# Hybrid decoder layer on one core: q and k blocks split in one operation and placed by DMA, weight sums by accumulating loads, gate and branch products in another order, output projection by single token tiles

## Chip, cores and metric

One core of one Trainium2 chip runs the whole layer. The metric is the device time of one execution in microseconds (us). Engines are named as in the profile: PE (TensorE), ACT (ScalarE), DVE (VectorE), POOL (GpSimd), SP (SyncE, which issues DMA transfers only here).

## The reference

One layer, float32, 512 tokens of width 1024, 256 memory tokens.

```
h = rms_norm(x, g_mix);  proj = h @ w_in            # q,k,v of two mixers, forget logits, memory q, 3 gates
y_m = moba_attention(rope(norm(q_m)), rope(norm(k_m)), v_m)     # 8 heads of 64, blocks of 256
y_f = fox_attention(norm(q_f), norm(k_f), v_f, cumsum(log_f))   # 8 heads of 64
y_c = memory_attention(norm(q_c), norm(k of mem), v of mem)     # 4 heads of 128
merged = sigmoid(a_m)*(y_m @ w_br_moba) + sigmoid(a_f)*(y_f @ w_br_fox) + sigmoid(a_c)*(y_c @ w_br_mem)
x = x + merged @ w_out
h2 = rms_norm(x, g_ffn)
x = x + (silu(h2 @ w_gate) * (h2 @ w_up)) @ w_down
```

With 512 tokens MoBA has two blocks, so its top-3 choice takes every past block and the attention is plainly causal.

## The kernel before

**Number format.** Every factor of a product is split into a high part, rounded to a narrow format on ACT (`w_hi`, `qT` first half), and a low part, the rest, by a subtraction on DVE (`w_lo`). A product is three matmuls (`PASSES`: high by high, high by low, low by high). q, k and v of the heads of 64 use another layout: a `qT` or `kT` slot holds high and low parts on two sets of 64 partitions, so that a score needs two matmuls over 128 partitions.

**Weights.** `pieces` lists the weight pieces of 512 x 256 (512 KB) in order of use. `load_next` (L161) loads one into a `w_raw` slot by SP; a piece of kind "pair" is loaded by SP and a second source is added onto it by an accumulating DMA that POOL issues (L169). The order of the loads is by `due`, or three pieces ahead (`RAW_AHEAD`). `split_next` (L185) makes the parts: the first `HALVES` (8) pieces in two halves, each with its own ACT and DVE operation, the later ones whole. `take` (L234) hands the split pieces to a product.

**Units by seven products.** Three units of 512 columns (K and Q of four MoBA heads, V, K and Q of the other four; `plan_unit`, L100) are computed by `tok_unit` (L666) in seven half-size products M1, M2, M5, M6, M3, M7, M4, whose left factors are weight pieces or sums of them: S1 is a "pair"; S2 (S1 plus the first piece of the unit) and S4 (S2 plus the second) are of kind "sum", added by DVE (`w_sum`, L197).

**Order of the work.** The order is written out by hand for all engines. PE's stream of large products passes through `mm` (L272); each time about 1.3 us of columns have been issued, `tick` (L257) puts the next bit of everything else into the queues: one weight split, the callbacks whose count has run out (`later(n, fn)`: n ticks), and steps of a list `side` at a given rate per tick (`beside(steps, rate)`). A `tick` comes after 7 matmuls of 512 columns or 13 of 256. `flush_side` (L279) runs all steps that are left, with no product between them; `branch_part` calls it when an attention's output is still missing.

**Heads.** After its product a group of four heads is normalised and rotated on POOL (`head_rest`), then `turn_pair` (L528) transposes a block of two heads into PSUM by four PE transposes, and evacuates it: ACT writes the high part of each head (L543, 64 partitions), DVE the low part of each (L547, 64 partitions). For q the four quarters lie crosswise in one slot; for k each head has a slot of its own, of which POOL doubles 64 partitions onto the other 64 by DMA a tick later (L551, L552). `attention` (L850) then runs 16 groups per call in steps: scores (PE, L858), negated minimum and mask (DVE, L869), exponential (ACT, L887), scaling of `p_t` (POOL, L891), transposes (PE, L909), split of `pt` (ACT L298, DVE L301), values (PE, L920), y (ACT L927, DVE L928), and, after the last of a pair, the split of `yT`. The memory attention (L776) is built alike; its scaling is at L804, its transposes at L815.

**Gates and branches.** `gate_part` (L983) computes a chunk of 256 gate columns and its tanh on ACT (with a load of ACT's function table, `use_table`, L63, where the set changes); `branch_part` (L993) projects the attention's output and multiplies; branch 1 adds to `acc` on POOL (L1012). `gate_chunk` is one after the other. The starts of the four attentions are the calls `later(n, lambda: beside(attention(...), rate))` at L1031, L1039, L1112 and L1122.

**Output projection.** For column chunks 0 and 1, `out_pair` (L1215) runs two token tiles at once, the last of the eight contraction tiles at the end, into two of the three "m" banks of PSUM; chunks 2 and 3 go by `out_group`. `out_sum` (L1205) adds x on DVE (L1208) and squares on ACT (L1210). The switch of the function table for the second norm stands ahead of it all (L1197). The feed-forward part behind it (L1153 to L1473) isn't touched.

Of the kernel before, what the change touches and what calls it, by code (L numbers as in the profile page):

```python
# [12 lines left out]
F32R = mybir.dt.float32r  # L13
# [6 lines left out]
NT = S // P  # L20
# [17 lines left out]
def f32(ap):  # L38
    return ap.bitcast(F32)
# [3 lines left out]
def hybrid_layer(ctx, tc, rope, x, mem, g_mix, w_in, b_forget, g_q_moba, g_k_moba, g_q_fox,  # L43
# [12 lines left out]
    def slot(name, dt=F32):  # L56
        return U.tile([P, SLOT], dt, name=name, tag="u", bufs=NSLOT)
# [42 lines left out]
    def plan_unit(col1, col2):  # L100

        i = len(pieces)
        a = {(c, kh): cols(w_in, kh, DIN, (col1, col2)[c], 256) for c in range(2) for kh in range(2)}
        pieces.extend([("load", a[0, 0], 4, 256), ("load", a[0, 1], 4, 256),
                       ("pair", (a[1, 0], a[1, 1]), 4, 256), ("sum", (i + 2, i), 4, 256),
                       ("sum", (i + 3, i + 1), 4, 256),
                       ("pair", (a[1, 0], a[0, 0]), 4, 256), ("load", a[1, 1], 4, 256)])
        due.update({i + 2: i - 5, i: i - 4, i + 1: i - 3, i + 5: i - 2, i + 6: i + 3})

    DIN = w_in.shape[2]  # L110
    for c in (0, 256):
# [12 lines left out]
    def plan_gates(a, wb, chunks):  # L124
        for c in chunks:
            plan_gate(a, c)
            plan_branch(wb, c)
# [10 lines left out]
    plan_cols(w_in, D, DIN, V_F + 256, 264)  # L138
    plan_cols(w_in, D, DIN, K_F + 256, 256)
    plan_cols(w_in, D, DIN, Q_F + 256, 256)  # L140
    plan_gates(A_M, w_br_moba, (0, 1))
    for b in (K_F, Q_F, V_F):
        plan_cols(w_in, D, DIN, b, 256)
    plan_gates(A_M, w_br_moba, (2, 3))
# [3 lines left out]

    raws, split, used = {}, {}, {}
    st = {"load": 0, "split": 0, "take": 0, "stage": 0}  # L150
    HALVES = 8
    RAW_AHEAD = 3
    loads = sorted((i for i, piece in enumerate(pieces) if piece[0] != "sum"),
                   key=lambda i: due.get(i, i - RAW_AHEAD))
# [6 lines left out]
    def load_next():  # L161
        i = loads[st["load"]]
        st["load"] += 1
        kind, src, nk, w = pieces[i]
        r = raws[i] = slot("w_raw")
        dst = r[:, :nk * w].rearrange("p (k c) -> p k c", k=nk)
        if kind == "pair":
            nc.sync.dma_start(dst, src[0])
            nc.gpsimd.dma_start(dst, src[1], accum_op=OP.add)  # L169
        else:  # L170
            nc.sync.dma_start(dst, src)

# [322 lines left out]
    def head_rest(raw, ss, ntok, d, kind, gc, dst, blk0, lag, rows=None, e=2, gains=None):  # L495
# [32 lines left out]
        def turn_pair(blk):  # L528
            tb = bank("a")
            for tt in range(ntok):  # L530
                pe.transpose(tb[:, tt * P:(tt + 1) * P],
                             raw[:, tt * 256 + blk * P:tt * 256 + (blk + 1) * P], ident)
            if gc in (GQM, GQF):
                o = slot("qT", F32R)
                dst[blk0 + blk] = o
                o2 = [(o[:, 0:512], o[:, 0:512]), (o[:, 512:1024], o[:, 512:1024])]
            else:
                ks = [slot("kT", F32R), slot("kT", F32R)]
                dst[blk0 + blk] = ks
                o2 = [(k[:, 0:512], k[:, 512:1024]) for k in ks]  # L540
            for h, (hi, lo) in enumerate(o2):
                r = slice(64 * h, 64 * h + 64)
                act.activation(hi[r], tb[r], AF.Copy, scale=g[r])  # L543
            for h, (hi, lo) in enumerate(o2):
                r = slice(64 * h, 64 * h + 64)
                q = slice(64 - 64 * h, 128 - 64 * h)
                dve.scalar_tensor_tensor(lo[q if gc in (GQM, GQF) else r], tb[r], g[r],  # L547
                                         f32(hi[r]), op0=OP.mult, op1=OP.subtract)
            if gc not in (GQM, GQF):
                def double():  # L550
                    nc.gpsimd.dma_start(ks[0][64:128, :1024], ks[0][0:64, :1024])  # L551
                    nc.gpsimd.dma_start(ks[1][0:64, :1024], ks[1][64:128, :1024])  # L552
                later(1, double)

        def turn(blk):
            if d == 64:
# [471 lines left out]
        gate_part(0, jc)  # L1028
    tok_unit((heads_of("rope", GKM, KM, 0), heads_of("rope", GQM, QM, 0, gneg)))
    tok_unit((values_of(VM, (0, 1)), values_of(VM, (2, 3))))  # L1030
    later(4, lambda: beside(attention((0, 1), QM, KM, VM, YM, None), 0.75))  # L1031
    for jc in (0, 1):
        branch_part(0, YC, jc)
    gate_chunk(0, YC, 2)
# [1 line left out]
    xf32.clear()  # L1036
    TH.clear()
    right_h.clear()
    later(17, lambda: beside(attention((2, 3), QM, KM, VM, YM, None, -1.0), 0.9))  # L1039
    gate_chunk(0, YC, 3)  # L1040


# [66 lines left out]
        load_bias(h)  # L1109
    for h in (4, 5, 6, 7):  # L1110
        later(h, lambda h=h: mask_bias(h))
    later(12, lambda: beside(attention((2, 3), QF, KF_, VF, YF, bias), 0.65))  # L1112
    for jc in (0, 1):
        gate_chunk(1, YM, jc)
    head_chunk(hT, NT, 64, "plain", GKF, KF_, 0)
    head_chunk(hT, NT, 64, "plain", GQF, QF, 0)
    for h in (0, 1, 2, 3):
# [1 line left out]
    v_chunk(VF, (0, 1))  # L1119
    for h in (0, 1, 2, 3):  # L1120
        later(h + 1, lambda h=h: mask_bias(h))
    later(4, lambda: beside(attention((0, 1), QF, KF_, VF, YF, bias), 1.0))  # L1122
    for jc in (2, 3):
        gate_chunk(1, YM, jc)

# [68 lines left out]
        gate_chunk(2, YF, jc)  # L1194


    use_table("natural_log_exp_and_others")  # L1197
    mgl = [mg[j] for j in range(KD)]
    x1 = []
    for t in range(NT):  # L1200
# [78 lines left out]
    for c in range(2):  # L1279
        Ws = take(2)  # L1280
        if c == 0:
            later(2, lambda: split_op(0, "M4", 1))
            later(4, lambda: sums(0, "S4"))
            later(6, lambda: split_op(0, "M7", 1))
        else:
            load_quarters(1, ("A11", "A12"))
            later(2, lambda: split_op(0, "M6", 1))
            later(5, lambda: split_op(0, "M3", 1))
        for t in range(0, NT, 2):
            out_pair(t, c, Ws)  # L1290
    W2, W3 = take(2), take(2)
    pace["ahead"] = 0
    for t in range(NT):
# [356 lines left out]
```

## Time and profile before

| | us |
|---|---|
| median of 3 runs | 875.71 (873.41 to 876.72) |
| the profiled execution | 875.18 |
| its span in the trace | 873.2 |
| PE busy in the span | 850.7 (97%), 5780 matmuls |
| DVE busy | 663.9 (76%) |
| ACT busy | 479.2 (55%) |
| POOL busy | 223.9 (26%) |
| mean granted PE clock | 0.997 of full speed |

The span is what the trace records of one execution; the time of the execution is 2.0 us more. Matmuls are pipelined and their ends are modelled, so the records of two matmuls overlap and a small wait between them does not show as idle.

### The profile page before, as it was taken

How to read it: one execution, taken by the hardware profiler on the slowest of the kernel's cores; microseconds unless marked ns; L12 is line 12 of the kernel's file. 1: busy time of each engine (PE TensorE's matmuls, PEld its weight loads, DVE VectorE, ACT ScalarE, POOL GpSimd, SP SyncE). 2: the span in 40 equal slices, each digit the busy share in tenths (PEclk: the TensorE clock that was granted, in tenths of full speed). 3: DMA queues.
4: the chain of work that ended last, by engine and by line, in shares of the span. 5: the costliest groups of instructions: out<-in, count | busy, mean ns of one | idle time of the engine just before them, and what ended most of it. 6: DMA issues, size and time to landing. Idle time of an engine off the chain costs nothing.

```text
span 873.2 us, 15224 instructions
## 1 busy us (share of the span) xinstructions
PE 850.7 (97%) x5780; PEld 782.3 (90%) x5780; DVE 663.9 (76%) x1172; ACT 479.2 (55%) x873; POOL 223.9 (26%) x310
## 2 busy tenths in 40 slices
PE   6999999999999999999999899999999999999998
PEld 6898998798899789988888899999999999988786
DVE  4988689768677666666555655889889898996985
ACT  7846665557767656666434445544433443574561
POOL 3212316212522451343310003222221222110220
PEclk9999999999999999999999999999999999999999
DMA  9924248126522521523692625698996889784992
GB/s 313 318 49 97 51 117 219 26 53 191 126 68 76 143 64 58 146 75 95 174 188 73 193 91 128 146 196 182 187 187 118 170 170 182 188 197 137 250 259 78
DMA packets 146264, 126.17 MB, mean 145 GB/s; under 512 B 5696, under 2 KB 130168, under 8 KB 146192
## 3 DMA queue, kind: packets, MB, share of 16 engines
q1 hardware_dynamic: 112816, 95.21, 37.4%
q0 software_dynamic: 32192, 27.89, 20.8%
q10 hardware_dynamic: 1184, 2.12, 0.7%
q8 instruction: 45, 0.74, 0.3%
q14 instruction: 27, 0.22, 0.1%
HBM read 116.79 MB, written 4.21 MB: 139 GB/s over the span
## 4 chain that ended last, share of the span: by engine, by line
PE 78%; DVE 10%; ACT 6%; issue 2%; DMA 2%; SPq 1%; ACTq 0%; POOL 0%; DVEq 0%; POOLq 0%
PE ps_m L276 36%; PE ps_a L1320 12%; PE ps_a L1473 10%; PE ps_m L1320 9%; PE ps_m L1473 3%; PE ps_a L920 2%; PE ps_a L858 2%; DVE w_lo L211 2%; PE ps_a L909 2%; ACT w_hi L208 2%; DMA x_t<-in_x_dram 1%; DVE wl L1179 1%; PE ps_a L783 1%; PE ps_a L826 1%; DVE xl L1265 1%
## 5 line engine op out<-in xcount | busy, mean ns | idle before, releaser
L211 DVE TENSOR_TENSOR w_lo<-w_raw,w_hi 128x1024 fp32r<-128x1024 f32 (+2 forms) x91 | 105.6, 1171 | 30.5 <-ACT w_hi L208 23.0
L276 PE MATMUL ps_m<-hT,w_hi 128*128 128x512 f32 x384 | 125.1, 401 | 0.0
L276 PE MATMUL ps_m<-w_hi,hT 128*128 128x256 f32 (+1 forms) x656 | 124.4, 285 | 0.0
L276 PEld LDWEIGHTS ps_m<-w_hi,hT 128*128 128x128 f32 x656 | 102.5, 189 | 0.2
L1320 PE MATMUL ps_a<-xh,wl 128*128 128x256 f32 x352 | 99.5, 283 | 1.0 <-DVE wl L1179 1.0
L1320 PE MATMUL ps_a<-xh,wh 128*128 128x256 f32 x352 | 99.2, 282 | 0.0
L1320 PE MATMUL ps_a<-xl,wh 128*128 128x256 f32 x352 | 99.0, 281 | 0.0
L276 PE MATMUL ps_m<-w_lo,hT 128*128 128x256 f32 (+1 forms) x328 | 93.9, 286 | 3.1 <-DVE w_lo L211 3.1
L208 ACT ACTIVATE w_hi<-w_raw 128x1024 fp32r<-128x1024 f32 (+2 forms) x91 | 86.9, 975 | 7.1 <-DMA w_raw<-in_w_mem_kv_dram 4.1
L276 PEld LDWEIGHTS ps_m<-hT,w_hi 128*128 128x128 f32 x384 | 71.7, 191 | 14.5
L1473 PE MATMUL ps_a<-dh,dr 128*128 128x512 f32 x242 | 77.5, 393 | 0.0
L276 PE MATMUL ps_m<-hT,w_lo 128*128 128x512 f32 x192 | 76.8, 400 | 0.0
L1320 PE MATMUL ps_m<-xl,wh 128*128 128x256 f32 x264 | 74.3, 281 | 0.0
L1320 PE MATMUL ps_m<-xh,wl 128*128 128x256 f32 x264 | 74.3, 281 | 0.0
L1320 PE MATMUL ps_m<-xh,wh 128*128 128x256 f32 x264 | 74.2, 281 | 0.0
L1153 POOL DMA_DIRECT2D wq<-in_w_gate_dram x22 | 34.1, 1551 | 154.3 <-DMA wq<-in_w_gate_dram 95.3
L891 POOL TENSOR_SCALAR p_t<-p_t,rc 128x128 f32<-128x128 f32 (+1 forms) x64 | 38.0, 594 | 128.6 <-DVE rc L890 109.1
L1179 DVE TENSOR_TENSOR wl<-wq,wh 128x1024 fp32r<-128x1024 f32 x55 | 66.8, 1218 | 3.2 <-ACT wh L1176 3.2
L1320 PEld LDWEIGHTS ps_a<-xh,wl 128*128 128x128 f32 x352 | 66.4, 189 | 1.6 <-DVE wl L1179 1.6
L1320 PEld LDWEIGHTS ps_a<-xh,wh 128*128 128x128 f32 x352 | 66.5, 189 | 0.0
L1320 PEld LDWEIGHTS ps_a<-xl,wh 128*128 128x128 f32 x352 | 66.4, 189 | 0.0
L276 PEld LDWEIGHTS ps_m<-w_lo,hT 128*128 128x128 f32 x328 | 61.9, 189 | 4.0 <-DVE w_lo L211 3.7
(271 smaller groups left out, 2261.4 us busy)
## 6 DMA issues: line engine op xcount, KB each, us to landing
w_raw<-in_w_in_dram SPq DMA_DIRECT2D x53, 512.0 KB, 3.8
wq<-in_w_gate_dram SPq DMA_DIRECT2D x55, 256.0 KB, 5.0
wq<-in_w_up_dram SPq DMA_DIRECT2D x55, 256.0 KB, 5.3
dq<-in_w_down_dram SPq DMA_DIRECT2D x25, 512.0 KB, 5.5
wq<-in_w_gate_dram POOLq DMA_DIRECT2D x22, 256.0 KB, 8.2
wq<-in_w_up_dram POOLq DMA_DIRECT2D x22, 256.0 KB, 10.2
dq<-in_w_down_dram POOLq DMA_DIRECT2D x10, 512.0 KB, 7.5
w_raw<-in_w_mem_kv_dram SPq DMA_DIRECT2D x8, 512.0 KB, 10.3
```

What stands on the lines that cost most here:

```text
L208: act.activation(hi[:, c], r[:, c], AF.Copy)
L211: dve.tensor_tensor(lo[:, c], r[:, c], f32(hi[:, c]), op=OP.subtract)
L276: pe.matmul(ps, lhsT, rhs, start=start, stop=stop)
L783: pe.matmul(ps[:, i2 * 256:(i2 + 1) * 256], QC[h][a][:, i * P:(i + 1) * P], KC[h][b], start=(a, b) == PASSES[0], stop=(a, b) == PASSES[-1])
L858: pe.matmul(ps[:, :n], Q[p][:, s * 512 + i * P:s * 512 + (i + 1) * P], K[p][s][:, b * 512:b * 512 + n], start=b == 0, stop=b == 1)
L891: pool.tensor_scalar(pt[:, :nk], pt[:, :nk], rc, 1.0, op0=OP.mult, op1=OP.mult)
L909: pe.transpose(tb[:, j * P:(j + 1) * P], pt[:, j * P:(j + 1) * P], ident)
L920: pe.matmul(yb[:, :256], V[p][:, j, 2 * s:2 * s + 2, :], PT[b][:, j, :], start=(j == 0 and b == 0), stop=(j == nj - 1 and b == 1))
L1153: e.dma_start(t[:, g * 512:(g + 1) * 512].rearrange("p (k c) -> p k c", k=4), dsrc(w, kh * 512 * DFF + f0 + fh * P, [[DFF, P], [P * DFF, 4 ...
L1179: dve.tensor_tensor(full(lo), full(r), f32(full(hi)), op=OP.subtract)
L1320: pe.matmul(ps[:, g * 256:(g + 1) * 256], w[a][:, g, k, :], r[b][:, k, :], start=n % 12 == 0, stop=n % 12 == 11)
L1473: pe.matmul(acc_d[m][t2], r[a][:, e * 256 + t2 * P:e * 256 + (t2 + 1) * P], w[b][:, e * 512:(e + 1) * 512], start=(p == 0 and e == 0 and ( ...
```

## The change

Six edits: the first 12 weight pieces are split in halves, not 8. S2 is loaded as a sum of three sources (one SP load and two accumulating POOL transfers into the same slot) instead of being added by DVE, with other due places for the loads. `turn_pair` evacuates both heads of a block in one ACT and one DVE operation over 128 partitions into a slot `qkT2`, and two ticks later SP places the parts by four transfers per block: 64 partitions x 512 for q, x 1024 for k. The gate parts of branch 1, chunks 0 and 1, go ahead of the branch parts. The four attentions start two or three ticks later, three of them at a higher rate. In the output projection only the first two token tiles of chunk 0 go as a pair, and the table switch moves behind chunks 0 and 1.

```diff
@@ -102,10 +102,11 @@
         i = len(pieces)
         a = {(c, kh): cols(w_in, kh, DIN, (col1, col2)[c], 256) for c in range(2) for kh in range(2)}
         pieces.extend([("load", a[0, 0], 4, 256), ("load", a[0, 1], 4, 256),
-                       ("pair", (a[1, 0], a[1, 1]), 4, 256), ("sum", (i + 2, i), 4, 256),
+                       ("add", (a[1, 0], a[1, 1]), 4, 256),
+                       ("add", (a[0, 0], a[1, 0], a[1, 1]), 4, 256),
                        ("sum", (i + 3, i + 1), 4, 256),
-                       ("pair", (a[1, 0], a[0, 0]), 4, 256), ("load", a[1, 1], 4, 256)])
-        due.update({i + 2: i - 5, i: i - 4, i + 1: i - 3, i + 5: i - 2, i + 6: i + 3})
+                       ("add", (a[1, 0], a[0, 0]), 4, 256), ("load", a[1, 1], 4, 256)])
+        due.update({i + 2: i - 4, i: i - 4, i + 1: i - 3, i + 3: i - 4, i + 5: i - 1, i + 6: i + 3})
 
     DIN = w_in.shape[2]
     for c in (0, 256):
@@ -138,7 +139,10 @@
     plan_cols(w_in, D, DIN, V_F + 256, 264)
     plan_cols(w_in, D, DIN, K_F + 256, 256)
     plan_cols(w_in, D, DIN, Q_F + 256, 256)
-    plan_gates(A_M, w_br_moba, (0, 1))
+    for c in (0, 1):
+        plan_gate(A_M, c)
+    for c in (0, 1):
+        plan_branch(w_br_moba, c)
     for b in (K_F, Q_F, V_F):
         plan_cols(w_in, D, DIN, b, 256)
     plan_gates(A_M, w_br_moba, (2, 3))
@@ -148,7 +152,7 @@
 
     raws, split, used = {}, {}, {}
     st = {"load": 0, "split": 0, "take": 0, "stage": 0}
-    HALVES = 8
+    HALVES = 12
     RAW_AHEAD = 3
     loads = sorted((i for i, piece in enumerate(pieces) if piece[0] != "sum"),
                    key=lambda i: due.get(i, i - RAW_AHEAD))
@@ -164,9 +168,10 @@
         kind, src, nk, w = pieces[i]
         r = raws[i] = slot("w_raw")
         dst = r[:, :nk * w].rearrange("p (k c) -> p k c", k=nk)
-        if kind == "pair":
+        if kind == "add":
             nc.sync.dma_start(dst, src[0])
-            nc.gpsimd.dma_start(dst, src[1], accum_op=OP.add)
+            for more in src[1:]:
+                nc.gpsimd.dma_start(dst, more, accum_op=OP.add)
         else:
             nc.sync.dma_start(dst, src)
 
@@ -530,27 +535,24 @@
             for tt in range(ntok):
                 pe.transpose(tb[:, tt * P:(tt + 1) * P],
                              raw[:, tt * 256 + blk * P:tt * 256 + (blk + 1) * P], ident)
+
+
+            both = slot("qkT2", F32R)
+            evac_split(both[:, 0:512], both[:, 512:1024], tb, g)
+            low, up = slice(0, 64), slice(64, 128)
             if gc in (GQM, GQF):
-                o = slot("qT", F32R)
-                dst[blk0 + blk] = o
-                o2 = [(o[:, 0:512], o[:, 0:512]), (o[:, 512:1024], o[:, 512:1024])]
+                o = dst[blk0 + blk] = slot("qT", F32R)
+                moves = [(o[r, 512 * s:512 * s + 512],
+                          both[(low, up)[s], 512 * a:512 * a + 512])
+                         for s in range(2) for a, r in enumerate((low, up))]
             else:
-                ks = [slot("kT", F32R), slot("kT", F32R)]
-                dst[blk0 + blk] = ks
-                o2 = [(k[:, 0:512], k[:, 512:1024]) for k in ks]
-            for h, (hi, lo) in enumerate(o2):
-                r = slice(64 * h, 64 * h + 64)
-                act.activation(hi[r], tb[r], AF.Copy, scale=g[r])
-            for h, (hi, lo) in enumerate(o2):
-                r = slice(64 * h, 64 * h + 64)
-                q = slice(64 - 64 * h, 128 - 64 * h)
-                dve.scalar_tensor_tensor(lo[q if gc in (GQM, GQF) else r], tb[r], g[r],
-                                         f32(hi[r]), op0=OP.mult, op1=OP.subtract)
-            if gc not in (GQM, GQF):
-                def double():
-                    nc.gpsimd.dma_start(ks[0][64:128, :1024], ks[0][0:64, :1024])
-                    nc.gpsimd.dma_start(ks[1][0:64, :1024], ks[1][64:128, :1024])
-                later(1, double)
+                ks = dst[blk0 + blk] = [slot("kT", F32R), slot("kT", F32R)]
+                moves = [(ks[s][r, :1024], both[(low, up)[s], :1024]) for s in range(2) for r in (low, up)]
+
+            def move():
+                for o, i in moves:
+                    nc.sync.dma_start(f32(o), f32(i))
+            later(2, move)
 
         def turn(blk):
             if d == 64:
@@ -1028,7 +1030,7 @@
         gate_part(0, jc)
     tok_unit((heads_of("rope", GKM, KM, 0), heads_of("rope", GQM, QM, 0, gneg)))
     tok_unit((values_of(VM, (0, 1)), values_of(VM, (2, 3))))
-    later(4, lambda: beside(attention((0, 1), QM, KM, VM, YM, None), 0.75))
+    later(6, lambda: beside(attention((0, 1), QM, KM, VM, YM, None), 0.8))
     for jc in (0, 1):
         branch_part(0, YC, jc)
     gate_chunk(0, YC, 2)
@@ -1036,7 +1038,7 @@
     xf32.clear()
     TH.clear()
     right_h.clear()
-    later(17, lambda: beside(attention((2, 3), QM, KM, VM, YM, None, -1.0), 0.9))
+    later(19, lambda: beside(attention((2, 3), QM, KM, VM, YM, None, -1.0), 1.0))
     gate_chunk(0, YC, 3)
 
 
@@ -1109,9 +1111,11 @@
         load_bias(h)
     for h in (4, 5, 6, 7):
         later(h, lambda h=h: mask_bias(h))
-    later(12, lambda: beside(attention((2, 3), QF, KF_, VF, YF, bias), 0.65))
+    later(15, lambda: beside(attention((2, 3), QF, KF_, VF, YF, bias), 0.7))
     for jc in (0, 1):
-        gate_chunk(1, YM, jc)
+        gate_part(1, jc)
+    for jc in (0, 1):
+        branch_part(1, YM, jc)
     head_chunk(hT, NT, 64, "plain", GKF, KF_, 0)
     head_chunk(hT, NT, 64, "plain", GQF, QF, 0)
     for h in (0, 1, 2, 3):
@@ -1119,7 +1123,7 @@
     v_chunk(VF, (0, 1))
     for h in (0, 1, 2, 3):
         later(h + 1, lambda h=h: mask_bias(h))
-    later(4, lambda: beside(attention((0, 1), QF, KF_, VF, YF, bias), 1.0))
+    later(7, lambda: beside(attention((0, 1), QF, KF_, VF, YF, bias), 1.0))
     for jc in (2, 3):
         gate_chunk(1, YM, jc)
 
@@ -1194,7 +1198,6 @@
         gate_chunk(2, YF, jc)
 
 
-    use_table("natural_log_exp_and_others")
     mgl = [mg[j] for j in range(KD)]
     x1 = []
     for t in range(NT):
@@ -1286,8 +1289,11 @@
             load_quarters(1, ("A11", "A12"))
             later(2, lambda: split_op(0, "M6", 1))
             later(5, lambda: split_op(0, "M3", 1))
-        for t in range(0, NT, 2):
-            out_pair(t, c, Ws)
+        if c == 0:
+            out_pair(0, c, Ws)
+        for t in range(2 * (c == 0), NT):
+            out_group(t, c, Ws)
+    use_table("natural_log_exp_and_others")
     W2, W3 = take(2), take(2)
     pace["ahead"] = 0
     for t in range(NT):
```

## Rows read from the trace of the kernel before

**Rows 1.** The view of waits of PE: what PE waited for; in all (us), how often, the longest.

```profile
PE ps_m L276 <- DVE w_lo L211: 5.0, 8, 1.3
```

**Rows 2.** The timeline of PE. Columns here and in all timelines: start (us), duration (us), engine, line, operation, output and inputs, form, how many in a run (x2: the duration is that of the run), and in brackets the idle time before it with what ended it.

```profile
40.66 0.28 PE L276 MATMUL ps_m<-w_hi,hT 128*128 128x256 f32 x1
40.78 0.28 PE L276 MATMUL ps_m<-w_lo,hT 128*128 128x256 f32 x1
43.34 0.39 PE L276 MATMUL ps_m<-w_lo,hT 128*128 128x256 f32 x1 [0.98 <-DVE w_lo L211]
138.24 0.39 PE L276 MATMUL ps_m<-w_lo,hT 128*128 128x256 f32 x1 [0.87 <-DVE w_lo L211]
155.35 0.70 PE L276 MATMUL ps_m<-yT,w_hi 128*128 128x512 f32 x2 [1.14 <-DVE raw L703]
201.10 0.39 PE L276 MATMUL ps_m<-w_lo,hT 128*128 128x256 f32 x1 [1.28 <-DVE w_lo L211]
291.42 0.39 PE L920 MATMUL ps_a<-pt,v 128*128 128x256 f32 x1 [0.34 <-ACT pt L298]
293.09 1.10 PE L920 MATMUL ps_a<-pt,v 128*128 128x256 f32 x7 [1.28 <-DVE pt L301]
370.30 1.10 PE L920 MATMUL ps_a<-pt,v 128*128 128x256 f32 x7 [0.31 <-DVE pt L301]
499.87 0.38 PE L276 MATMUL ps_m<-w_hi,mg 128*128 128x256 f32 x1 [2.43 <-DVE x L1208]
518.05 0.39 PE L276 MATMUL ps_m<-w_lo,mg 128*128 128x256 f32 x1 [0.42 <-DVE w_lo L211]
```

**Rows 3.** The view by windows, 290 to 300 us: length, busy time and count of PE, its weight loads, DVE, ACT and POOL, then the granted clock of PE, the DMA share and GB/s.

```profile
290.00:300.00 10.00, 8.38 (x43) 6.90 (x42) 4.75 (x11) 3.66 (x8) 8.40 (x11) 0.83 0.61 159
```

**Rows 4.** The timeline of DVE around 42 us.

```profile
42.07 1.22 DVE L211 TENSOR_TENSOR w_lo<-w_raw,w_hi 128x1024 fp32r<-128x1024 f32 x1
```

**Rows 5.** The timeline of DVE in the second unit of seven products.

```profile
129.00 1.22 DVE L197 TENSOR_TENSOR w_sum<-w_raw 128x1024 f32<-128x1024 f32 x1
134.08 1.75 DVE L197 TENSOR_TENSOR w_sum<-w_sum,w_raw 128x1024 f32<-128x1024 f32 x1
```

**Rows 6.** The timeline of DVE, then of ACT, in the third unit.

```profile
194.78 1.22 DVE L197 TENSOR_TENSOR w_sum<-w_sum,w_raw 128x1024 f32<-128x1024 f32 x1
197.43 1.04 ACT L208 ACTIVATE w_hi<-w_sum 128x1024 fp32r<-128x1024 f32 x1
```

**Rows 7.** The accumulating loads (line L169): shortest, median and longest time from issue to landing.

```profile
DMA to landing us min/median/max: 6.0/6.4/7.3
```

**Rows 8.** The timelines of SP, POOL and PE around 95 to 102 us.

```profile
94.51 0.37 SPq L171 DMA_DIRECT2D w_raw<-in_w_in_dram  x1
97.95 1.83 POOL L804 TENSOR_SCALAR p_t<-p_t,rc 128x256 f32<-128x256 f32 x2 [2.72 <-DVE rc L801]
101.25 0.60 PE L815 MATMUL ps_a<-ident,p_t 128*128 128x128 f32 x4
```

**Rows 9.** Groups of instructions by line and form: line, engine, operation, output and inputs, form, count; busy us and mean ns of one; idle before.

```profile
L543 ACT ACTIVATE kT<-ps_a,gcol 64x512 fp32r<-64x512 f32 x16 | 10.9, 682 | 7.0 <-PE ps_a L531 6.8
L547 DVE SCALAR_TENSOR_TENSOR kT<-ps_a,gcol,kT 64x512 fp32r<-64x512 f32 x16 | 12.0, 749 | 5.5 <-ACT kT L543 5.0 <-issue 0.3
L306 DVE SCALAR_TENSOR_TENSOR hT<-ps_a,gcol,hT 128x512 fp32r<-128x512 f32 x8 | 5.6, 746 | 0.4 <-ACT hT L303 0.4
```

**Rows 10.** The timeline of DVE around 153 us.

```profile
152.55 1.51 DVE L547 SCALAR_TENSOR_TENSOR qT<-ps_a,gneg,qT 64x512 fp32r<-64x512 f32 x2
```

**Rows 11.** The timelines of ACT and DVE around 290 us.

```profile
290.77 0.98 ACT L298 ACTIVATE pt<-ps_a 128x512 fp32r<-128x512 f32 x2
289.71 1.52 DVE L547 SCALAR_TENSOR_TENSOR kT<-ps_a,gcol,kT 64x512 fp32r<-64x512 f32 x2
```

**Rows 12.** The timeline of SP around 490 us: issues of DMA transfers; one issue, at 489.51, lies between these two.

```profile
489.09 0.37 SPq L1153 DMA_DIRECT2D wq<-in_w_gate_dram  x1
490.10 0.46 SPq L1153 DMA_DIRECT2D wq<-in_w_gate_dram  x1
```

**Rows 13.** The timelines of DVE and PE where the second MoBA attention begins.

```profile
239.61 1.53 DVE L547 SCALAR_TENSOR_TENSOR qT<-ps_a,gneg,qT 64x512 fp32r<-64x512 f32 x2
243.86 0.40 PE L858 MATMUL ps_a<-kT,qT 128*128 128x256 f32 x2
```

**Rows 14.** The doubling of k by POOL (line L551): shortest, median and longest time from issue to landing.

```profile
DMA to landing us min/median/max: 2.8/3.2/6.7
```

**Rows 15.** The timeline of PE where the first MoBA attention begins: its first scores.

```profile
157.74 0.40 PE L858 MATMUL ps_a<-kT,qT 128*128 128x256 f32 x2
```

**Rows 16.** The timeline of DVE at the end of the last FoX attention.

```profile
431.05 0.69 DVE L301 TENSOR_TENSOR yT<-y,yT 128x512 fp32r<-128x512 f32 x1 [0.70 <-ACT yT L298]
```

**Rows 17.** The timelines of ACT and DVE in the first chunk of the output projection.

```profile
492.46 1.28 ACT L63 ACT_TABLE_LOAD   x1
493.76 2.01 ACT L208 ACTIVATE w_hi<-w_raw 128x1024 fp32r<-128x1024 f32 x2
499.40 0.75 DVE L1208 TENSOR_TENSOR x<-ps_m,x 128x256 f32<-128x256 f32 x2
```

**Rows 18.** The view by windows, two stretches of 5 us (columns as in Rows 3).

```profile
141.00:146.00 5.00, 5.00 (x45) 5.00 (x45) 3.57 (x5) 2.83 (x5) 4.38 (x6) 1.00 1.07 212
240.00:245.00 5.00, 5.00 (x44) 5.00 (x43) 4.03 (x12) 1.83 (x6) 0.00 (x0) 1.00 0.47 95
```

## Prediction

> **What bounds the kernel now.** The page comes first: TensorE (PE) is busy 97% of the span, VectorE (DVE) 76%, ScalarE (ACT) 55%, and the change leaves PE's 5780 matmuls as they are. So it can only move PE's gaps, and the waits of PE are the next view: the largest sum is 5.0 us on DVE's w_lo [rows 1]. The timeline of PE gives each gap its place [rows 2]. An idle entry understates the loss: matmuls of 256 columns begin 0.12 us apart but are recorded as 0.28 long (its first two rows), so each gap cost its idle plus about 0.16. As lost time, the gaps that the change can touch are 1.14 (at 43), 1.03 (138), 1.30 (155), 1.44 (201), 0.50 and 1.44 (291, 293), 0.47 (370), 2.59 (500) and 0.58 (518): 10.5 us in all. Behind the gap at 293 the clock cost more: the view by windows has 0.83 of full speed granted in 290 to 300 [rows 3], between the levels 1.2 and 2.4 GHz, and 0.17 of 10 us is 1.7 us. All together, 12.2 us, is what removing these waits could give at most: 875.7 - 12.2 = 863.5.
>
> Durations come from the profiled execution, 875.18 us (span 873.2, and 2.0 around it). The median of the runs is 875.71, 0.5 more; I take the sum off the median.
>
> **The change, part by part.**
>
> *Pieces 8 to 11 split in halves.* At 43 PE waits for the low half of a weight piece split as a whole, 1.22 on DVE from 42.07 [rows 4], behind its w_hi on ACT. In halves, the first w_lo covers 512 columns, about 0.6 us, and can start some 0.5 sooner; the second follows, and there are more instructions in both queues. Between 0 and 1.1 I take **+0.6**.
>
> *S2 by accumulating DMA instead of by DVE (three units).* It takes one 1.2 us addition per unit off DVE. In the second unit that is the one at 129.00, at the head of the chain whose 1.75 us addition at 134.08 [rows 5] holds the w_hi and w_lo that PE awaits at 138. 1.2 us covers that 1.03 and part of a smaller gap at 134: **+1.3** (0.5 to 1.4). In the third unit the addition at 194.78 can run a tick sooner; its w_hi on ACT stood at 197.43 [rows 6], behind exponentials, so an earlier sum lets it stand ahead of them: **+1.4** (0 to 1.44).
> The price is on POOL's queue, which is in order. An accumulation takes 1.3 us there and lands 6.4 us after its issue (6.0 to 7.3) [rows 7], and the second into one buffer must wait for the first. In the second unit the loads fall due in the tick of SP's issue at 94.51, and the scaling of p_t of the memory attention, then at 97.95, is behind them; PE transposes its result at 101.25 [rows 8]. With both at 94.3 POOL is free at 94.3 + 6.4 + 1.3 = 102.0, and p_t is done about 1 us later: **-1.7** (0 if POOL gets there sooner, -5 if SP's load in front is late as well). In the first and third unit I find no work of POOL's that waits.
>
> *One evacuation per block.* On 64 partitions ACT takes 0.68 and DVE 0.75 for each half, and the same width on 128 partitions takes DVE 0.75 as well [rows 9]: 16 x 0.68 us go on ACT, 16 x 0.75 on DVE. At 155 DVE held two such operations, 1.51 us, ahead of the raw for which PE waited [rows 10]: **+0.8** (0 to 1.3). At 291 and 293 both engines are in the chain: ACT's pt at 290.77 follows kT, table load and tanh, DVE's pt follows kT, 1.52 at 289.71 [rows 11]. ACT comes some 0.7 sooner, which ends the 0.50; DVE 0.75 and what ACT gave, so 1.0 of the 1.44. What stays is shorter than the idle 1.28 at 201, after which the clock held, so I let the 1.7 go with it: **+3.2** (0.5, if the clock falls all the same, to 3.6). At 370: **+0.4** (0 to 0.47).
> Each block is then placed by four SP transfers, 64 in all, 12.6 MB in place of POOL's sixteen of 256 KB. SP's issues are 0.5 apart [rows 12]. The attentions start two or three ticks later; a tick is 7 matmuls of 512 or 13 of 256 columns, 1.6 us. The tight place is the second MoBA attention: its first scores ran at 243.86, block 0's evacuation on DVE at 239.61 [rows 13]. Its moves go from about 241, the scores to 245.8. The last issue at 241 + 3 x 0.5, with the old copies' median landing of 3.2 [rows 14], ends at 245.7; with a little for SP's wait for DVE **-0.5** (0 to -5). In the first MoBA attention the scores go from 157.74 [rows 15] to 161.7, the moves from about 153: 8.6 us. Loads that SP issues behind a move wait with it; they run ahead of their use, so 0 (to -2, one wait on w_lo as at 201).
>
> *Gate parts ahead of branch parts.* The same operations in another order; the first branch comes later, so no flush falls into it, and POOL's additions to acc bunch behind the second. 0 (-0.5 to 0.5).
>
> *Last FoX attention three ticks later at the same rate.* Its last step now comes due three matmuls after branch F0 begins, so the branch flushes it with nothing beside it: y copied and added on ACT and DVE, yT on ACT and then on DVE, 0.69 for the last [rows 16] and about 0.5 for each other, as for the pt of rows 11 (0.98 for two). 2.2 less some 0.8 for three matmuls and ends that overlap: **-1.4** (0, to -4 if the clock falls as after 293).
>
> *Output projection by single groups, table load moved.* At 500 PE waited for x, which DVE did at 499.40, at the end of a chain that began with a table load at 492.46 and two w_hi [rows 17]. 1.28 off that chain and three matmuls (0.36) before the bank is needed give +1.6. The load now stands ahead of the w_hi whose w_lo PE awaited at 518.05, with 0.58 lost there already: 1.28 less a little that ACT was idle, -1.1. Net **+0.5** (-1 to 1.6). The next activation is at 493.76, 0.02 behind the load's end, so the rows show 1.28 and no more. The Trainium skill, "ScalarE: Activation LUTs", What ACT_TABLE_LOAD costs, puts a drain of 1.38 us on top of each; by that page this part would be -0.9 and the sum 872.5, but this trace does not agree.
>
> *Rates 0.75 to 0.8, 0.9 to 1.0, 0.65 to 0.7.* The later starts are made up for, the steps end in the same ticks: 0 (-1 to 0, as the steps are denser).
>
> **Sum**: 0.6 + 1.3 + 1.4 - 1.7 + 0.8 + 3.2 + 0.4 - 0.5 - 1.4 + 0.5 = 4.6; 875.71 - 4.6 = **871.1**.
>
> **The rivals.** *A, slower: the moves land late.* Place: the first scores of both MoBA attentions. The DMA engines were full at 141 to 146, where the first one's K blocks go (share 1.07), and half used at 240 to 245 [rows 18]. Of the old copies one landed after 6.7 us [rows 14]. In the second attention the last of four would then land at 241 + 1.5 + 6.7 = 249.2, 3.4 late; in the first, moves that take 12 us are 3.4 late. With 1.7 each for the clock that is 10.2, and loads held behind the moves make two or three w_lo late by 1.3: 3.5. With the 0.5 of the forecast taken back, 871.1 - 0.5 + 13.7 = 884. It decides from a landing of 4.8 us in the second and 8.6 in the first; above 880.1 it is from 9.5 us lost. For it: no slack at 245.8; against: the queue of the second one is half empty. Chance 0.16.
>
> *B, no change: the new waits eat the gains.* POOL's block costs 5 instead of 1.7, or the flush brings the slow clock and 4 instead of 1.4: 874.4 or 873.7, and 877.0 with both; I take 875. For it: p_t ran just ahead of its use at 101; against: either hangs on one place. Chance 0.16.
>
> *C, no change: the relief only moves gaps.* ACT's exponentials, not DVE, end the denser attentions' waits, so that half of the 8.2 us of gains stays: 875.2. For it: the w_hi at 197.43 waited on ACT. Against: 5.0 us of waits name DVE. Chance 0.08.
>
> *D, much faster.* The gains reach their upper ends, 1.1 + 1.4 + 1.4 + 1.3 + 3.6 + 0.5 + 1.6 = 10.9, and POOL, moves and flush find their cover: 865. Chance 0.12.
>
> **How the numbers follow.** The forecast has 0.48, with its own range 868 to 873.5. A measurement of this kernel can tell about 0.5%, 4.4 us: faster lies below 871.3, slower above 880.1. Of the forecast's 0.48, some 0.31 lies below 871.3, as the bounds at 293, 201 and 500 reach further down than up; with D faster has 0.43. Its other 0.17 with B and C is 0.41 for no change, and A the 0.16 for slower. The range leaves out A and the half of D that goes lowest: 865.5 to 877.5.
>
> **What would show it.** In the new profile: PE's waits on w_lo near 2 us, not 5.0; no wait on raw at 155; full clock in 290 to 300; a new wait of about 1.7 near 102 whose chain leads to POOL's p_t; one on yT near 434; on x at 500 about 1, and on w_lo near 518 1.5. Wrong would be: scores that wait for a DMA (A), an unchanged gap at 293 (ACT alone set it), or no gap near 102 (the loads come at another time than I read).

## The result and the profile after

The changed kernel took 880.86 us (median of five runs, 877.64 to 881.23) against 875.71: a ratio of 1.0053 with a 95% interval of 1.003 to 1.0076. It is slower by half a per cent, just above the 880.1 from which the prediction calls it slower, and 3.4 us above its range. The profiled execution took 881.2 us with a span of 879.5, 6.3 more than before.

The view of waits of PE, changed kernel (in all, how often, longest), to set beside [rows 1]:

```profile
PE ps_a L817 <- POOL p_t L806: 3.9, 1, 3.9
PE ps_a L860 <- DMA qT<-qkT: 3.5, 1, 3.5
PE ps_m L281 <- DVE w_lo L216: 2.5, 5, 0.9
PE ps_m L281 <- ACT yT L303: 0.9, 1, 0.9
PE ps_m L281 <- ACT w_hi L213: 0.8, 2, 0.6
PE ps_m L281 <- DVE x L1211: 0.6, 1, 0.6
PE ps_a L922 <- DVE pt L306: 0.6, 1, 0.6
```

The waits on w_lo fell from 5.0 to 2.5 us, that on x from 2.4 to 0.6, that on raw at 155 is gone. At the top stand two that were not there: 3.9 us on POOL's p_t and 3.5 us on a move of q. The timeline of PE gives their places, to set beside [rows 2]:

```profile
42.54 0.38 PE L281 MATMUL ps_m<-w_lo,hT 128*128 128x256 f32 x1 [0.45 <-DVE w_lo L216]
104.45 0.92 PE L817 MATMUL ps_a<-ident,p_t 128*128 128x128 f32 x2 [3.89 <-POOL p_t L806]
105.81 0.41 PE L281 MATMUL ps_a<-w_lo,xh 128*128 128x256 f32 x1
106.02 0.41 PE L281 MATMUL ps_a<-w_hi,xl 128*128 128x256 f32 x1
168.04 0.47 PE L860 MATMUL ps_a<-kT,qT 128*128 128x256 f32 x2 [3.48 <-DMA qT<-qkT]
296.62 0.86 PE L922 MATMUL ps_a<-pt,v 128*128 128x256 f32 x5 [0.56 <-DVE pt L306]
438.69 0.51 PE L281 MATMUL ps_m<-yT,w_hi 128*128 128x512 f32 x1 [0.91 <-ACT yT L303]
439.41 0.50 PE L281 MATMUL ps_m<-yT,w_hi 128*128 128x512 f32 x1 [0.22 <-DVE yT L306]
503.49 0.39 PE L281 MATMUL ps_m<-w_hi,mg 128*128 128x256 f32 x1 [0.64 <-DVE x L1211]
521.38 0.39 PE L281 MATMUL ps_m<-w_hi,mg 128*128 128x256 f32 x1 [0.64 <-ACT w_hi L213]
522.70 0.39 PE L281 MATMUL ps_m<-w_lo,mg 128*128 128x256 f32 x1 [0.93 <-DVE w_lo L216]
```

The view by windows behind the gaps, with the granted clock in the column after POOL's; the third is to set beside [rows 3]:

```profile
104.00:110.74 6.74, 6.29 (x26) 5.83 (x27) 1.55 (x3) 2.45 (x6) 4.76 (x9) 0.50 0.77 139
165.00:172.00 7.00, 3.96 (x13) 3.32 (x14) 3.44 (x7) 1.50 (x4) 1.28 (x1) 0.77 0.91 207
290.00:300.00 10.00, 9.44 (x55) 7.94 (x54) 7.84 (x16) 7.41 (x15) 6.05 (x9) 1.00 0.70 170
521.00:527.00 6.00, 4.69 (x25) 4.49 (x26) 2.70 (x3) 1.79 (x4) 0.00 (x0) 0.73 0.07 22
```

Three of the new gaps left the clock at its lower level for a while: at 104 to 110.74 it is 0.50, and matmuls of 256 columns begin 0.21 us apart (105.81, 106.02) instead of 0.12. That loses some 0.44 of the 6.3 us behind the gap. Matmuls found in both traces give the whole loss at this place: PE was 0.84 us ahead of the kernel before at the last scores in front of the gap (99.69 against 100.53) and 6.2 behind at 112.10 (105.89 there). That is 7.0, of which 4.0 is the gap itself and 3.0 the clock.

With idle plus 0.16 for each gap, as before, and the slow stretches beside them:

| place in the kernel before | before, us | after, us |
|---|---|---|
| 43, w_lo | 1.1 | 0.6 |
| 100, p_t of the memory attention | 0 | 4.0, clock 3.0 |
| 134 and 138, w_lo of the second unit | 1.4 | 0 |
| 155, raw | 1.3 | 0 |
| first scores of the first MoBA attention | 0 | 3.6, clock 1.6 |
| 196 and 201, third unit | 1.8 | 0 |
| 291 and 293, clock | 1.9, 1.7 | 0.7 |
| 370, pt | 0.5 | 0 |
| branch F0, yT | 0 | 1.5 |
| 500, x | 2.6 | 0.8 |
| 518, w_lo and w_hi | 0.6 | 1.9, clock 1.5 |
| sum | 12.9 | 19.2 |

The sum grew by 6.3, as much as the spans differ; the idle of the gaps not listed, at the start and in the feed-forward part, is 0.6 us less after (8.3 against 8.8), so the account closes to within 0.6. The change did what it was forecast to do at most gaps; two of its prices were far too low, and the output projection lost instead of gaining.

**The first price, POOL.** The timeline of POOL, changed kernel:

```profile
88.81 0.93 POOL L806 TENSOR_SCALAR p_t<-p_t,rc 128x256 f32<-128x256 f32 x2 [8.60 <-DVE rc L803]
91.14 0.93 POOL L806 TENSOR_SCALAR p_t<-p_t,rc 128x256 f32<-128x256 f32 x2 [1.40 <-DVE rc L803]
92.01 2.60 POOL L174 DMA_DIRECT2D w_raw<-in_w_in_dram  x2
102.60 1.28 POOL L174 DMA_DIRECT2D w_raw<-in_w_in_dram  x1 [7.99 <-DMA w_raw<-in_w_in_dram]
103.39 3.21 POOL L806 TENSOR_SCALAR p_t<-p_t,rc 128x256 f32<-128x256 f32 x6
```

The two operations in the row of 92.01 are the accumulations of S1 and the first of S2, in flight together; the second of S2, at 102.60, waited 7.99 us of idle for the landing. Behind it six scalings of p_t stood in line at 103.39, of which the kernel before had the middle pair at 97.95 [rows 8]; PE's transposes went at 104.45. The first pair of the six is the one that PE needed first, at 100.4. The kernel before had it at 94.30 (timeline of POOL, kernel before):

```profile
94.30 0.93 POOL L804 TENSOR_SCALAR p_t<-p_t,rc 128x256 f32<-128x256 f32 x2 [1.42 <-DVE rc L801]
```

The landing took longer than the 6.4 of [rows 7], some 9.5 us, on DMA engines that the added loads kept busy: the windows of 92 to 102.6, first the changed kernel, then the kernel before, have a DMA share of 0.87 and 0.21.

```profile
92.00:102.60 10.60, 8.56 (x73) 8.36 (x72) 7.19 (x13) 6.80 (x18) 2.61 (x3) 1.00 0.87 150
92.00:102.60 10.60, 10.60 (x90) 10.50 (x90) 7.36 (x13) 7.53 (x20) 4.57 (x8) 1.00 0.21 53
```

**The second price, the moves.** The timeline of SP, and as the last row that of DVE, changed kernel:

```profile
147.32 0.37 SPq L176 DMA_DIRECT2D w_raw<-in_w_in_dram  x1
148.46 11.87 SPq L554 DMA_DIRECT2D kT<-qkT  x8
160.43 4.90 SPq L554 DMA_DIRECT2D qT<-qkT  x4
156.91 0.75 DVE L311 SCALAR_TENSOR_TENSOR qkT<-ps_a,gneg,qkT 128x512 fp32r<-128x512 f32 x1 [2.41 <-ACT qkT L308]
```

Eight moves of k took SP 11.87 us to issue, 1.5 each and not the 0.5 of [rows 12]; the first q block, whose evacuation was at 156.91, was issued only from 160.43 on, 4.9 us for four, and PE had its scores ready to go at 164.4 and began at 168.04. The DMA share of these 15 us goes with it: first the changed kernel, 150 to 165, then the kernel before, 146 to 161, the same stretch of its work (its k blocks are evacuated from 144.0 on, 147.7 in the changed kernel).

```profile
150.00:165.00 15.00, 14.46 (x75) 11.58 (x73) 10.02 (x18) 6.40 (x12) 3.34 (x3) 1.00 1.09 218
```

```profile
146.00:161.00 15.00, 13.86 (x74) 11.42 (x73) 14.71 (x23) 8.27 (x15) 2.90 (x4) 1.00 0.71 140
```

The DMA share went from 0.71 to 1.09. The accumulating loads suffered too (line L174, issue to landing, with [rows 7] to compare):

```profile
DMA to landing us min/median/max: 6.0/7.3/15.4
```

### The profile page after: what moved, and what is told of

Same layout as the page of the kernel before. It is cut to its first block, busy times and chain, and to the rows that moved or that the text cites. A ratio compares the mean times of both kernels' runs of the same rounds, so it can differ in the third digit from the quotient of the medians.

```text
span 879.5 us, 15281 instructions
## 1 busy us (share of the span) xinstructions
PE 855.4 (97%) x5780; PEld 786.3 (89%) x5780; DVE 648.4 (74%) x1157; ACT 467.1 (53%) x861; POOL 223.4 (25%) x300
## 4 chain that ended last, share of the span: by engine, by line
PE 80%; DVE 8%; ACT 5%; DMA 3%; issue 1%; SPq 1%; POOL 1%; ACTq 0%; DVEq 0%; POOLq 0%
PE ps_m L281 37%; PE ps_a L1326 12%; PE ps_a L1479 10%; PE ps_m L1326 9%; PE ps_m L1479 3%; PE ps_a L922 2%; PE ps_a L860 2%; PE ps_a L911 2%; DMA x_t<-in_x_dram 1%; DVE w_lo L216 1%; PE ps_a L281 1%; DMA w_raw<-in_w_in_dram 1%; DVE wl L1183 1%; ACT w_hi L213 1%; PE ps_a L828 1%
## 5 line engine op out<-in xcount | busy, mean ns | idle before, releaser
L216 DVE TENSOR_TENSOR w_lo<-w_raw,w_hi 128x1024 fp32r<-128x1024 f32 (+2 forms) x98 | 111.1, 1145 | 31.5 <-ACT w_hi L213 25.3
L213 ACT ACTIVATE w_hi<-w_raw 128x1024 fp32r<-128x1024 f32 (+2 forms) x98 | 90.8, 945 | 16.9 <-DVE w_lo L216 8.3
L1369 ACT ACTIVATE z<-z 128x512 f32<-128x512 f32 x22 | 13.9, 633 | 93.5 <-DVE z L705 93.5
```

The lines of the kernel that those rows point to most:

```text
L213: act.activation(hi[:, c], r[:, c], AF.Copy)
L216: dve.tensor_tensor(lo[:, c], r[:, c], f32(hi[:, c]), op=OP.subtract)
L1369: act.activation(z[:, :, 0, :], z[:, :, 0, :], AF.Silu, scale=1.0 - 2 * j)
```

## The experiments

All of them are compared with the kernel before on the same chip (874.8 to 875.6 there, 875.71 in the comparison of the changed kernel). Against the changed kernel and between chips the ratios are therefore safer than the medians; where the two differ, both are given. A trace shows one execution, and the clock did not fall alike in all executions of a kernel.

**e1, S2 of the second unit as before.**

```diff
-    plan_unit(V_M, V_M + 256)
+    plan_unit(V_M, V_M + 256, True)   # ... pieces and due places of the kernel before
```

> The changed kernel, with the weight sum S2 of the second unit alone (the V unit) loaded and added as before (one accumulating load, DVE adds). Theory: in the changed kernel POOL stood behind two accumulating loads from 92 to 102.6 us, PE lost 4.4 us at 100 to 104 and some 2.6 more to the slow clock behind it. Without it 7.0 come back, less the waits on w_lo at 134 and 138 that the sum on DVE brings again (1.4): 880.9 - 5.6 = 875.3, and no wait of the memory attention's transposes. Rival: POOL only showed a shortage of DMA; then the wait stays at 2 us or more and the time at 878 to 881.

Measured 876.14, ratio 1.0019 (1.0007 to 1.0032): 4.7 less than the changed kernel by the medians, 3.0 by the ratios, 5.6 forecast. The wait on p_t is gone, those on w_lo at 134 and 138 are back; the q move is as late as before (timeline of PE, e1):

```profile
164.28 0.77 PE L867 MATMUL ps_a<-kT,qT 128*128 128x256 f32 x2 [3.63 <-DMA qT<-qkT]
```

In this execution the clock was slow for longer behind the wait (6.8 us instead of 3.4). It was the longest of the ten, 879.14 at a mean clock of 0.994; the other nine had 0.995 to 1.000, so this does not tell why the median gained less than 5.6. The waits themselves show that the accumulation ahead of p_t is the first cause, and that the second is independent of it.

**e2, S2 of all three units as before.** The same edit on all three `plan_unit` calls.

> The changed kernel with S2 of all three units by DVE as before. Theory that the q moves of the first MoBA attention were late because they stand behind SP's eight k moves on full DMA engines: two accumulations and a load less in 150 to 167 bring them forward, PE's wait for qT at 164 (3.66 and some 1.5 by the clock) goes to under 1 us, and the waits on w_lo of the third unit come back (1.4 to 1.8): 875.3 - 5 + 1.6 = 872. Rival, that SP's order alone makes them late: the wait at 164 stays at over 2.5 us and the time is 877.

It takes a load of 512 KB and two accumulations of as much out of each unit. Measured 872.42, ratio 0.9971 (0.9957 to 0.9985), the time that the theory had (872), though one term of its sum did not come (below). The wait for qT is gone altogether. By the window of 145 to 160, the same stretch of the work in e2:

```profile
145.00:160.00 15.00, 14.91 (x79) 12.26 (x78) 12.70 (x22) 7.30 (x13) 1.29 (x1) 1.00 0.90 224
```

the DMA share is 0.90 against 1.09. The part of the theory that said the third unit's waits would come back failed: no gap of PE over 0.3 us stands between 154 and 285 in e2. What took them away was not S2.

**e3, q moves from ACT's queue.**

```diff
+            queue = nc.scalar if gc in (GQM, GQF) else nc.sync
-                    nc.sync.dma_start(f32(o), f32(i))
+                    queue.dma_start(f32(o), f32(i))
```

> The changed kernel with the q moves issued from ACT's DMA queue, the k moves on SP as they are. Rival theory (SP's order): q moves no longer stand behind the k moves, which SP issued 2 us apart; the wait at 164 goes, 880.9 - 5 = 876. Theory of full DMA engines: the q packets share the engines with the k moves and land after 164 all the same, wait 2 us or more, 879 to 881.

Measured 881.37, ratio 1.008 (1.005 to 1.011), no better than the changed kernel. On a queue of their own the q moves land no sooner (timeline of PE, then of ACT, e3):

```profile
166.50 0.77 PE L862 MATMUL ps_a<-kT,qT 128*128 128x256 f32 x2 [4.33 <-DMA qT<-qkT]
158.85 0.42 ACT L724 ACTIVATE v<-raw 128x256 fp32r<-128x256 f32 x1 [1.86 <-DMA kT<-qkT]
158.88 3.76 ACTq L556 DMA_DIRECT2D qT<-qkT  x4
```

4.33 us of wait. ACT's queue had itself waited for moves of k to land when it came to the q moves at 158.88, so e3 takes away SP's order but not every tie to the k moves. From there the scores still waited 7.6 us, where they waited for nothing in e2, which issued the moves at 156.19 for scores at 159.25. So SP's order alone did not make the moves late. With e1, where the wait stayed, e2 shows what did: the load and two accumulations of S2 that fill the DMA engines in the third unit (e2 takes out the first unit's as well, whose work is done by then).

**e4, the old evacuation in the changed kernel** (`turn_pair` of the kernel before, k doubled by POOL).

> The changed kernel with the old evacuation of q and k (two operations of 64 partitions per engine, k doubled by POOL's DMA). Theory: the wait for qT at 164 goes (-5.2), the waits at 155 (1.3), 291 to 300 (about 3.0 with the clock) and 370 (0.5) come back: 880.9 - 0.4 = 880.5. Rival, that one evacuation gains nothing because the denser attentions cover DVE anyway: 876.

Measured 884.89, ratio 1.0124 (1.0108 to 1.0139): 4 slower than the changed kernel by the medians, 6 by the ratios; both expectations missed. The timeline of PE, and as the last row that of POOL, e4:

```profile
159.65 0.70 PE L281 MATMUL ps_m<-yT,w_hi 128*128 128x512 f32 x2 [1.19 <-DVE raw L708]
167.36 0.47 PE L863 MATMUL ps_a<-kT,qT 128*128 128x256 f32 x2 [1.91 <-DMA kT<-kT]
296.77 0.98 PE L925 MATMUL ps_a<-pt,v 128*128 128x256 f32 x3 [2.36 <-DVE pt L306]
369.41 0.52 PE L914 MATMUL ps_a<-ident,p_t 128*128 128x128 f32 x3 [1.52 <-DVE kT L552]
375.43 0.36 PE L281 MATMUL ps_m<-w_hi,hT 128*128 128x256 f32 x1 [1.01 <-DVE v L306]
158.40 1.28 POOL L174 DMA_DIRECT2D w_raw<-in_w_in_dram  x1 [6.36 <-DMA w_raw<-in_w_in_dram]
```

The wait on raw is back (1.19), the wait for q at 164 is replaced by one for POOL's doubling of k (1.91), whose issues stood behind 6.36 us of POOL's wait for an accumulation, and with the denser attentions DVE's two evacuations hold pt, k and v up at 294 to 375 for longer than they did before. The single evacuation is worth more in this kernel than the gaps of the kernel before showed: 4 to 6 us, with its late moves still counted against it.

**f1, the evacuation alone.** The kernel before with the new `turn_pair` and the four changed starts and rates.

> The kernel before with the single evacuation of q and k blocks and SP's moves alone, with the changed starts and rates of the four attentions; weight loads, sums, gates and output projection as before. Theory: this part alone takes away the waits at 155 (1.3), 291 to 300 (3.0 with the clock) and 370 (0.5); since the third unit's waits on w_lo (1.8) stayed away in e2 although DVE added there, they go too; the flush at branch F0 costs 1.6: 875 - 6.6 + 1.6 = 870. Rival, that the moves find no room on the DMA engines without the other parts either: a wait for qT at 160 of 2 us or more, 874.

Measured 872.29, ratio 0.9961 (0.9948 to 0.9973): faster than before, between the two expectations. No wait for a q move is in its trace, and no gap over 0.3 us from 155 to 285. The moves find room when POOL's extra accumulations are not there. Against g3 below, which has the starts and rates alone, the single evacuation is worth some 6 us.

**f2, e2 with the last FoX attention after 4 ticks** (`later(7, ...)` back to `later(4, ...)`).

> e2 with the last FoX attention started after 4 ticks, as before, and not after 7. Theory: its last step comes ahead of branch F0, the waits on yT at 428 (1.05 and 0.5) go: 872.4 - 1.6 = 870.8. Rival: the earlier start finds q moves that have not landed at 365 to 375, and a wait of 1 us or more stands there: 872 to 874.

Measured 872.04, ratio 0.9966 (0.9952 to 0.998): the same as e2. The waits on yT at 428 are gone, and a wait for a move stands at 376 (timeline of PE, f2):

```profile
376.51 0.47 PE L867 MATMUL ps_a<-kT,qT 128*128 128x256 f32 x2 [1.58 <-DMA qT<-qkT]
```

The rival was right: with 4 ticks the moves have too little time, with 7 the end is flushed.

**f3, e2 with the table load at its old place.**

> e2 with the table load back ahead of the output projection, the single groups kept. Theory: the load costs 1.28 in either place: the wait on x at 493 grows from 0.8 to about 2.1, those at 511 and 512 (0.8 and 1.2) shrink to about 0.6: 872.4 and no change within 0.5. Rival by the rule of a drain behind each switch: with ACT busier at 511 than at 493 the old place is the better one by over 1.4: 871.

Measured 871.74, ratio 0.9956 (0.994 to 0.9972), no difference that these intervals show. The timeline of PE and the window behind the first gap, f3:

```profile
495.21 0.58 PE L288 MATMUL ps_m<-w_hi,mg 128*128 128x256 f32 x1 [2.06 <-DVE x L1219]
514.45 0.39 PE L288 MATMUL ps_m<-w_lo,mg 128*128 128x256 f32 x1 [0.42 <-DVE w_lo L223]
494.00:500.00 6.00, 4.79 (x28) 4.79 (x29) 3.25 (x6) 2.25 (x7) 0.00 (x0) 0.72 0.00 0
```

The waits went where they were expected, 2.06 on x and 0.42 on w_lo. That 2.06 brought the slow clock with it (0.72 in 6 us), where the 2.43 of the kernel before [rows 2] did not.

**f4, e2 with S2 of the second unit by later accumulating loads.**

```diff
-        due.update({... i + 3: i - 4, ...})
+        due.update({... i + 3: i - 1, ...})
```

> e2, but with S2 of the second unit by two accumulating loads again, its load due three pieces later than in the changed kernel, so that POOL has most scalings of the memory attention's p_t ahead of it. Theory: only POOL's order made this part costly; the wait at 100 stays away and the waits on w_lo at 133 and 136 (1.45 together) go: 871. Rival, that the accumulation itself is too slow: the block moves to the next p_t or S2 is late, with a wait of 2 us or more: 874 or above.

Measured 871.04, ratio 0.9949 (0.9933 to 0.9965). The waits of the second unit are gone, and the block moved to the end of the memory attention (timeline of PE, f4):

```profile
119.95 0.77 PE L824 MATMUL ps_a<-ident,p_t 128*128 128x128 f32 x2 [1.48 <-POOL p_t L813]
```

1.48 us there, so the gain over e2 is inside the intervals. The price of an accumulation is where POOL has to wait for it.

**g1 and g2, the best of both.** On e2 and on f4: the last FoX attention after 5 ticks, the table load between the first two chunks of the output projection.

> e2 (all S2 by DVE) with the last FoX attention after 5 ticks in place of 7, and the table load between the first two chunks of the output projection. Theory: the waits on yT at 428 (1.55) go without a new one for qT at 374 (f2, after 4 ticks, had 1.74 there), and the load at about 500 falls into ACT's idle time, so that the waits at 511 and 512 (2.0) shrink to 0.6: 872.4 - 1.5 - 1.4 = 869.5. Rival: the flush stays or the wait for qT comes, 871; or the load only moves the wait, 871.

> f4 (S2 of the second unit by two later accumulating loads) with the same two edits as g1. Theory: as f4 stood to e2 (-1.4 at 133 and 136, +2.7 at 118 and 160 in the trace), it stands to g1: between 869 and 870.5. Rival, that less DVE work in the second unit pays beyond its gaps: 868.

g1 measured 867.39, ratio 0.9913 (0.9899 to 0.9928); g2 868.55, ratio 0.9927 (0.9912 to 0.9942). g1 beats both kernels, by 8.2 us the one before and by 12 (ratios) to 13.5 (medians) the changed one. The largest waits on DVE and ACT that its view of PE's waits has are these, and the waits behind the table load at 512 and 513 (0.65 and 0.93 in e2) are down to one of 0.38 (the load itself: timeline of ACT, second fence):

```profile
PE ps_m L288 <- DVE w_lo L223: 3.1, 7, 0.9
PE ps_a L1333 <- DVE wl L1190: 1.1, 3, 0.5
PE ps_m L288 <- DVE x L1218: 0.6, 1, 0.6
```

```profile
497.25 1.28 ACT L63 ACT_TABLE_LOAD   x1
498.54 1.06 ACT L220 ACTIVATE w_hi<-w_raw 128x1024 fp32r<-128x1024 f32 x1
```

No wait on yT and none for a q move is left. g2 came out between its expectation (869 to 870.5) and its rival (868). That g1 won 5 us on e2, where 3 was expected, is only partly explained by its gaps: the two profiled executions differ by 3.0, e2's median is above its own (870.4), and e2 had a pt wait of 0.9 at 354 that g1 has at 0.5.

**g3, starts and rates alone.** The kernel before with only the four changed calls of `later` and `beside`.

> The kernel before with the four attentions' changed starts and rates alone. It tells what took the third unit's waits on w_lo (1.8 at 196 and 199) away, which S2 by DMA was forecast to do, but which stayed away in e2 and f1 as well. If it is the place of the attention's steps: they are gone here too, and with the flush (1.6) at branch F0 the time is 875 - 1.8 + 1.6 = 875. If it is the single evacuation: they stay, 876.5.

Measured 878.22, ratio 1.0038 (1.0024 to 1.0052), slower than both expected. The third unit's waits on w_lo are gone here, too, so the place of the attention's steps took them away, neither S2 nor the evacuation. What the denser steps cost in return is at 291 (timeline of PE, g3), 2.35 where it was 1.28, with another 1.8 lost at 368:

```profile
291.31 1.01 PE L920 MATMUL ps_a<-pt,v 128*128 128x256 f32 x3 [2.35 <-DVE pt L301]
```

**g4, e2 with the old order of gates and branches.**

> e2 with the old order of gate and branch parts of the MoBA branch, chunks 0 and 1. Theory: the order is worth nothing as long as the attention's end is covered, 872.4 within 0.6. Rival: with the attention two ticks later its last step falls into the branch, a flush of 1 to 2 us at 286 to 295: 874.

Measured 870.32, ratio 0.9944 (0.9928 to 0.996) against e2's 0.9971 (0.9957 to 0.9985). Both expectations missed (872.4 within 0.6, and 874). No flush at the branch; if anything the old order is a little better. The intervals overlap, so only that no gain of the new order shows can be said.

## Why the prediction was wrong

**Right.** The bound and the method: PE's gaps make the whole difference (6.3 of 6.3 us in the profiled executions). Of the gains at 43, 138, 155, 291, 370 and 500, each came within half a microsecond: 0.5 for the 0.6 forecast, 1.4 for 1.3, 1.3 for 0.8, 2.9 for 3.2, 0.5 for 0.4, 1.8 for 1.6. The flush at F0 cost 1.5 for the 1.4 forecast.

**Wrong in size, the first step that failed: POOL's queue.** It was taken at 1.7 with a bound of 5 and measured 7.0. The mechanism was the right one: in e1 the wait is gone. The term took a landing of 6.4 for one accumulation; in the changed kernel two were in flight together, it took some 9.5, and the second of S2 was let go at 102.6, while PE needed p_t at 100.4. That made 4.0. The other 3.0 is the clock, which the sum had priced in the bounds of the flush and the moves but not here. That the wait came at the forecast place is in part chance: the pair of scalings that PE transposes at 101.25 is the third, at 94.30 in the kernel before, and not the one at 97.95. With the loads behind the third pair, as forecast, POOL free at 102.0 would have been in time for the fourth, which PE took at 105.33. The loads came at 92.01, ahead of the third pair.

**Wrong, the second step: the 8.6 us of the first MoBA attention.** The sum put all risk of the moves (-0.5) on the second MoBA attention, which shows no wait at all, and nothing on the first, which lost 3.6 and 1.6. The error was to count the 8.6 from the evacuation on, as if the moves went at once: the eight k moves in front took 11.87 us of SP with the DMA share at 1.09, so that the q moves went 2.8 us after their evacuation was done. They had 4.0 us left to 164.4, and the scores began 7.6 after their issue. Rival A had this place and nearly this price (3.4 and 1.7), and had the full engines in its row of 141 to 146; its other half, the second attention and held loads, did not come. What it lacked was that the change itself adds the traffic: in the third unit S2 by accumulation, in the same 15 us. Each part was costed against the trace of before, not against the other part: the moves alone (f1) and the DVE sums with the moves (e2) both gain, and e2 against e1, 3.7 us on one chip, is the price of S2 by accumulation in the first and third unit together.

**Wrong in sign, a small one: output projection.** Forecast +0.5; the wait on x gave 1.8, but the table load at its new place cost 1.3 in gaps, where 1.1 was forecast, and 1.5 in clock, where nothing was: -1.0 together. The table load took 1.28 with the next activation 0.01 behind it (518.98, 520.27 in the trace), so no drain shows here either.

**Right by chance: the third unit.** +1.4 was forecast for S2; 1.8 came, from the place of the attention's steps (g3), and S2 there only cost. The starts and rates themselves, put at 0 apart from the flush, are not free: alone they made the kernel 2.6 us slower (g3, flush included), as the denser steps met the two evacuations at 291 and 368. With the single evacuation these two waits are 0.6 and none (f1).

With these three terms as measured (7.0 for 1.7, 5.2 for 0.5, 1.0 lost for 0.5 gained) the sum of 4.6 becomes -6.9; with 0.4 more in the third unit and 0.5 more at 155 it is -6.0, against -6.3 between the two spans and -5.2 between the medians.

## What to carry to other kernels

Where a change adds work to a resource in two places, cost the parts together in the window where both fall: here the moves had room without the accumulating loads (f1, e2), and not with them. An operation that waits for a DMA on an in-order queue costs the time to its landing, for everything behind it (POOL idled 7.99 us); look at what is queued there and when it is next needed, match each row to the operation that uses it, and allow for the clock behind a new gap: here it cost 1.5 to 3.0 us behind three of them. A single operation over 128 partitions in place of two over 64 was worth taking here although its outputs had to be moved, where the moves had room (f1).

## What the runs showed of the hardware

The length of a gap did not tell whether the clock fell: 2.43 us on x left it at full speed in the kernel before, 2.06 at the same place lowered it in f3. Waits of 0.64 and 0.93 us, 1.3 us apart, lowered it in the changed kernel (521 to 527), and the same two (0.65 and 0.93 at 512 and 514) did not in e2. Nor was it alike in each execution: the mean clock of the ten executions of e1 went from 0.994 (879.1 us) to 1.000 (873.7 us). The waits for q of 3.5 to 4.3 us lowered it each time (after, e1, e3), for 3.4 or 6.8 us; the wait on p_t lowered it where it was 3.9 (after), and not where it was 3.3 (e3). An issue on SP, 0.5 us apart at [rows 12], took up to 2.58 us in the stretch with a DMA share above 1 (line L554's issues: 0.46 to 2.58 over the whole trace), and moving it to ACT's queue put these issues into ACT's way instead (3.76 us for four at 158.88 in e3).
